# Half of the second key copy left out: fixed key tiles with zeroed rows in a two-layer hybrid decoder trunk

## The chip, the cores and the metric

The kernel runs on one core of one Trainium2 chip, in one launch. The metric is device time in microseconds (us). The time before is 1172.51 us, the median of three runs.

## The reference, cut to what matters

The model is a decoder trunk of two layers over 512 tokens of width 1024. In each layer an RMSNorm is followed by one input projection that feeds a short convolution, a causal differential attention and a Conformer convolution; their outputs are joined by an output projection, and a SwiGLU network follows. The change touches the attention alone. It has 4 heads, and each head has two maps (`m`) of 64-wide queries and keys:

```python
q = apply_rope(q.reshape(b, s, 2, N_DIFF_HEADS, DIFF_HEAD_DIM), cos, sin)
k = apply_rope(k.reshape(b, s, 2, N_DIFF_HEADS, DIFF_HEAD_DIM), cos, sin)
...
sc = jnp.einsum("bqmhd,bkmhd->bmhqk", qi, k, preferred_element_type=jnp.float32) * scale
p = jax.nn.softmax(jnp.where(mask, sc, -jnp.inf), axis=-1)
a = p[:, 0] - lam * p[:, 1]
return jnp.einsum("bhqk,bkhe->bqhe", a.astype(v.dtype), v)
```

Everything is float32. The kernel gets near that precision by splitting a factor into a high part (rounded to the matmul's own input type) and a low part (what the rounding left), and by adding products of the parts.

## The kernel before, in words

The activations lie transposed, 128 channels on the partitions by 512 tokens. Weights come from HBM in units of 512 KB (`raw`), each in two halves. ScalarE (ACT) copies a half to its high part, and the low part comes from VectorE (DVE, line 144 or 154) or, in the attention stretch, from ACT writing minus the high part (line 137) and a DMA from GpSimd (POOL, line 138) that adds the weights to it from HBM a second time. In that stretch POOL also issues the unit loads (line 118). Every engine works in the order in which the program names its instructions (`manual_schedule`), so a cast that waits for its weights holds back all that stands behind it on ACT.

The four heads go in two pairs, per layer. For each pair the projections give two PSUM tiles of queries (two halves of the rotary dimension, `ab`), then two of keys. `turn_qk` applies the rotary tables `cosr` and `sinr` on DVE; `split_and_pack` splits each result into the high and the low part (`hl`, 128 partitions by 2 by 512) and moves blocks of 32 partitions with DMAs from SyncE (SP) into the layout that the score matmuls want, line 450 for queries (`pq`) and line 448 for keys (`pk`). A pack is 16 DMAs in the order head of the pair (`hh`), `ab`, map (`m`), copy (`d`). Of a head's query tile the partitions 0 to 63 hold the high part and 64 to 127 the low part. Of a head's key tile both halves of the partitions hold the same: for each map a row group of high parts (`2 * m`) and one of low parts (`2 * m + 1`). So two matmuls give all four products (lines 489 and 490), and a third adds the causal mask (491):

```python
T.matmul(ps[:, m, :n], lhsT=q[:, m, qs], rhs=k[:, 2 * m, :n], start=True, stop=False)
T.matmul(ps[:, m, :n], lhsT=q[:, m, qs], rhs=k[:, 2 * m + 1, :n], start=False, stop=False)
```

There are four key packs in the program: layer 0 pair 0, layer 0 pair 1, layer 1 pair 0, layer 1 pair 1. Behind the keys of pair 0 comes the value projection (`values`): it fills four PSUM banks, ACT takes them out into `vt` (line 467), and the first scores of pair 0 need those banks. Behind the keys of pair 1 come the units of the short convolution (tiles `ax`, `ac`, `ab`) as filler, and the first scores of pair 1 need the first head's 8 DMAs of the pack. `slot` mixes scores, softmax, value products and two filler steps by hand.

At the start of the program POOL issues four DMAs that fetch `cosr` (line 697); DVE multiplies it by the norm's factor (line 703) before the first queries are turned.

Of the kernel before, what the change touches and what calls it, by code (L numbers as in the profile page):

```python
# [19 lines left out]
F32 = mybir.dt.float32  # L20
F32R = mybir.dt.float32r
# [7 lines left out]
S = 512  # L29
L = 2  # L30
P = 128
# [4 lines left out]
HD = 64  # L36
# [42 lines left out]
def trunk(ctx, tc, xT, pos, wu, cv, lamv, cst, out):  # L79
    nc = tc.nc  # L80
    V, A, G, T = nc.vector, nc.scalar, nc.gpsimd, nc.tensor

    def pool(name, bufs, **kw):
        return ctx.enter_context(tc.tile_pool(name=name, bufs=bufs, **kw))
    cp = pool("cp", 1)
# [4 lines left out]
    pk = pool("pk", 2)  # L90
# [125 lines left out]
    def start():  # L216


        nc.sync.dma_start(cvt, cv)
        nc.sync.dma_start(x[0], xT[0])  # L220
        load(0)
        nc.sync.dma_start(x[1], xT[1])
        load(1)
        nc.sync.dma_start(x[2], xT[2])
        nc.sync.dma_start(x[3], xT[3])
        load(2)
        nc.sync.dma_start(x[4], xT[4])
        ones_d = cp.tile([P, P], F32, name="ones_d")
        pi = pt.tile([P, P], I32, tag="t", name="posi")
        G.dma_start(pi, pos)  # L230
        lv = pt.tile([P, L, 4, HD], F32, tag="t", name="lv")
        G.dma_start(lv, lamv.partition_broadcast(P))
        G.dma_start(ones_d, cst[:, 1, :])
        cs = pt.tile([P, 2, P], F32, tag="t", name="cs")
        G.dma_start(cs, cst[:, 0::2, :])
        warm = sm.tile([P, 1], F32, tag="nm", name="warm")
        V.memset(warm, 0.0)
        A.activation(warm, warm, AF.Sin)

        wz = pt.tile([P, S], mybir.dt.bfloat16, tag="t", name="wz")  # L240
        V.memset(wz, 0.0)
        wp = tp.tile([P, S], F32, tag="tp", name="wp")
        for _ in range(10):
            T.matmul(wp, lhsT=wz[:, :P], rhs=wz, start=True, stop=True)
        ones_r = cp.tile([P, P], F32R, name="ones_r")
        idr = cp.tile([P, P], F32R, name="idr")
        maskr = cp.tile([P, P], F32R, name="maskr")
        G.tensor_copy(ones_r, ones_d)
        G.tensor_copy(idr, cs[:, 0, :])
        G.tensor_copy(maskr, cs[:, 1, :])  # L250
        consts.update(ones_d=ones_d, ones_r=ones_r, idr=idr, maskr=maskr, ident=idr.bitcast(F32), pi=pi, lv=lv)
# [6 lines left out]
    def make_h(k, gcol):  # L258

        g = cvt[:, gcol + k:gcol + k + 1]  # L260
        h = ph.tile([P, 2, S], F32R, tag="h", name=f"h{k}")
        A.activation(h[:, 0, :], x[k], AF.Copy, scale=g)  # L262
        V.scalar_tensor_tensor(h[:, 1, :], x[k], g, h[:, 0, :].bitcast(F32), ALU.mult, ALU.subtract)  # L263
        return h

    def add_square(k, run, eng, last=None):
        if run is None:
            run = pt.tile([P, S], F32, tag="t", name="run")
            A.activation(run, x[k], AF.Square)
            return run  # L270
        sq = pt.tile([P, S], F32, tag="t", name="sq")
        A.activation(sq, x[k], AF.Square)
        (V if (k == KC - 1 if last is None else last) else eng).tensor_add(run, run, sq)
        return run
# [69 lines left out]
    def rope_tables():  # L344

        p1, p2, p3 = _parts()
        w = pt.tile([P, 3, P], F32, tag="t", name="rt")
        ang, k, kl = (w[:, i, :] for i in range(3))
        kt = pt.tile([P, 3, P], F32R, tag="t", name="kh")
        kh = kt[:, 0, :]  # L350
        tab = kt[:, 1:3, :].bitcast(F32)
        cn, sn = tab[:, 0, :], tab[:, 1, :]
        V.tensor_copy(ang, consts["pi"])
        V.tensor_scalar(ang, ang, cvt[:, C_INV:C_INV + 1], None, ALU.mult)
        V.tensor_scalar(k, ang, 1.0 / TWO_PI, MAGIC, ALU.mult, ALU.add)
        V.tensor_scalar(k, k, -MAGIC, None, ALU.add)
        V.tensor_copy(kh, k)
        V.tensor_sub(kl, k, kh.bitcast(F32))
        yield
        for kk, p in ((kh.bitcast(F32), p1), (kl, p1), (kh.bitcast(F32), p2), (kl, p2), (k, p3)):  # L360
            V.scalar_tensor_tensor(ang, kk, -p, ang, ALU.mult, ALU.add)
        V.tensor_scalar(ang, ang, 3.1415925, -3.1415925, ALU.min, ALU.max)
        V.scalar_tensor_tensor(kl, ang, -1.0, ang, ALU.mult, ALU.min)
        yield
        A.activation(sn, ang, AF.Sin)
        A.activation(cn, kl, AF.Sin, bias=half_pi)
        dr = tc.dram_tile([32, 2, 4, P], F32, name="tab_dram")
        for b in range(4):
            (G, nc.sync)[b % 2].dma_start(dr[:, :, b, :], tab[32 * b:32 * b + 32, :, :])
        yield dr  # L370
# [14 lines left out]
            yield  # L385

    pending = []
    gates = []

    def later():  # L390
# [18 lines left out]
    def turn_qk(isk, ps, cosr, sinr, packs):  # L409

        t = [pt.tile([P, S], F32, tag="t", name=f"ro{i}") for i in range(4)]
        V.tensor_mul(t[0], ps[0], cosr)
        V.tensor_mul(t[1], ps[0], sinr)
        yield
        V.tensor_mul(t[2], ps[1], sinr)
        V.tensor_mul(t[3], ps[1], cosr)
        V.tensor_sub(t[0], t[0], t[2])
        V.tensor_add(t[1], t[1], t[3])
        if not packs:
            packs += [[pk.tile([P, n, S], F32R, tag=tag, name="p" + tag) for tag, n in (("q", 2), ("k", 4))]  # L420
                      for _ in range(2)]
        pending.append(functools.partial(split_and_pack, isk, t, packs))
        yield

    def split_and_pack(isk, t, packs):
        hls = [pr.tile([P, 2, S], F32R, tag="hl", name="hl") for _ in range(2)]
        for ab in range(2):
            if isk:
                A.copy(hls[ab][:, 0, :], t[ab])
            else:  # L430
                A.mul(hls[ab][:, 0, :], t[ab], QS)
        for ab in range(2):
            o, hl = t[ab], hls[ab]
            if isk:
                V.tensor_sub(hl[:, 1, :], o, hl[:, 0, :].bitcast(F32))
            else:
                V.scalar_tensor_tensor(hl[:, 1, :], o, QS, hl[:, 0, :].bitcast(F32), ALU.mult, ALU.subtract)
        for hh in range(2):
            q, k = packs[hh]
            for ab in range(2):  # L440
                hl = hls[ab]
                for m in range(2):
                    src = slice(64 * hh + 32 * m, 64 * hh + 32 * m + 32)
                    for d in range(2):
                        dst = slice(64 * d + 32 * ab, 64 * d + 32 * ab + 32)
                        eng = nc.sync
                        if isk:
                            eng.dma_start(k[dst, 2 * m:2 * m + 2, :].bitcast(F32), hl[src].bitcast(F32))
                        else:
                            eng.dma_start(q[dst, m, :].bitcast(F32), hl[src, d, :].bitcast(F32))  # L450

# [190 lines left out]
    def mixing(l, h, run, each):  # L642
# [3 lines left out]
        packs = [[], []]  # L646


        pq = [acc.tile([P, S], F32, tag="acc", name="qk") for _ in range(2)] if l == 0 else []
        pp = four("cc")  # L650

        def chunks(ks):
            for k in ks:
                w = next_half() if l else None
                for j, ps in enumerate(pq + pp):
                    c = slice(j * P, j * P + P)
                    mm3(ps, h[k], k == 0, k == KC - 1, w and (w[:, 0, c], w[:, 1, c]))
        if l == 0:
            start()

            hs = []

            def chunk(k):
                h.append(make_h(k, C_MIXG))
                if k:
                    hs.append(add_square(k - 1, hs[-1] if hs else None, V, True))
            rt = rope_tables()
            next(rt)
            prep(0, False)
            chunk(0)  # L670
            prep(1, False)
            chunk(1)
            next(rt)
            lam = lambdas()
            for k in range(6):
                lead[0] = (1, 2, 2, 3, 3, 3)[k]
                chunks([k])
                if k < 3:
                    nc.sync.dma_start(x[k + 5], xT[k + 5])
                chunk(k + 2)  # L680
                if k == 0:
                    state["tab"] = next(rt)
                if k == 1:
                    next(lam)
            hs.append(add_square(KC - 1, hs[-1], V, True))
            run = hs[-1]
            lead[0] = AHEAD - 1
        else:
            chunks(range(6))
# [237 lines left out]
    for l in range(L):  # L927
# [24 lines left out]
        for half in range(2):  # L952
            acts = []
            for f in range(FH):
# [8 lines left out]
                t = pt.tile([P, S], F32, tag="t", name="tg")  # L963
# [128 lines left out]
```

## Time and profile before

| | |
|---|---|
| median of 3 runs | 1172.51 us (1172.22 to 1177.48) |
| the profiled execution's own time | 1169.26 us |
| its span | 1167.4 us |
| PE (matmul) busy | 1137.1 us, 97% |
| DVE, ACT, POOL busy | 637.2, 502.6, 198.5 us |
| mean granted TensorE clock | 0.986 |
| DMA | 141.68 MB, mean 121 GB/s |

The profiled execution has 1.9 us outside its span. A busy share of 97% on PE counts the instructions from start to modelled end, at whichever clock they ran. The granted clock is 1.00 for 2.4 GHz and 0.50 for 1.2 GHz.

### The profile page before, as it was taken

The numbers are of one execution on the slowest core, as the hardware profiler recorded it, in microseconds if no ns is written. First come the engines' busy times: TensorE is split into PE (matmuls) and PEld (weight loads), VectorE is DVE, ScalarE is ACT, GpSimd is POOL, SyncE is SP. The second block draws the span as 40 slices with busy tenths as digits, with TensorE's granted clock in tenths as the row PEclk, the third lists the DMA queues.
The fourth block names the chain that finished last, engine by engine and source line by source line (L and its number), as shares of the span: only waits on it lengthen the run. The fifth ranks groups of instructions, "written<-read, shape, count | busy, mean of one in ns | idle before, by whom it ended". The sixth has DMA issues, their size and how long they took to land.

```text
span 1167.4 us, 14339 instructions
## 1 busy us (share of the span) xinstructions
PE 1137.1 (97%) x5238; PEld 943.8 (81%) x5238; DVE 637.2 (55%) x1140; ACT 502.6 (43%) x1034; POOL 198.5 (17%) x229
## 2 busy tenths in 40 slices
PE   8989899999999999999999899999999999999995
PEld 6878787788888888888888788877888888888885
DVE  6777786654443344444448788657444333444445
ACT  6546566643332233333334467765333222333323
POOL 2222223311100011010112222332111000011001
PEclk9989899999999999999999899999999999999998
DMA  7785847432332322322337878663223223223212
GB/s 228 190 211 130 197 109 165 106 126 91 104 95 90 109 91 94 105 90 99 102 98 177 195 170 190 139 158 97 102 90 106 93 91 108 91 94 105 90 55 73
DMA packets 50342, 141.68 MB, mean 121 GB/s; under 512 B 7104, under 2 KB 9408, under 8 KB 50272
## 3 DMA queue, kind: packets, MB, share of 16 engines
q1 hardware_dynamic: 29888, 88.79, 23.7%
q0 software_dynamic: 20384, 51.98, 19.5%
q8 instruction: 41, 0.67, 0.2%
q14 instruction: 29, 0.24, 0.1%
HBM read 125.93 MB, written 2.23 MB: 110 GB/s over the span
## 4 chain that ended last, share of the span: by engine, by line
PE 85%; DMA 4%; DVE 4%; issue 3%; ACT 2%; SPq 1%; POOL 1%; DVEq 0%; ACTq 0%; POOLq 0%
PE od L186 8%; PE od L188 8%; PE od L187 8%; PE gp L188 7%; PE gp L187 7%; PE up L187 7%; PE up L188 7%; PE up L186 7%; PE gp L186 6%; PE qk L186 3%; DMA raw<-wu 2%; PE qk L187 2%; PE qk L188 2%; PE cc L186 1%; PE cc L187 1%
## 5 line engine op out<-in xcount | busy, mean ns | idle before, releaser
L135 ACT CAST w<-raw 128x512 fp32r<-128x512 f32 x384 | 237.6, 622 | 495.1 <-PE od L188 146.0
L144 DVE TENSOR_TENSOR w<-raw,w 128x512 fp32r<-128x512 f32 x265 | 187.1, 707 | 239.8 <-ACT w L135 239.2
L966 POOL TENSOR_TENSOR tg<-tg,r 128x512 f32<-128x512 f32 x44 | 57.8, 1316 | 520.3 <-ACT tg L965 510.7
L187 PE MATMUL gp<-h,w 128*128 128x512 f32 x352 | 137.2, 390 | 0.6 <-DVE h L263 0.6
L186 PE MATMUL up<-h,w 128*128 128x512 f32 x352 | 137.2, 390 | 0.1
L188 PE MATMUL gp<-h,w 128*128 128x512 f32 x352 | 137.1, 390 | 0.0
L186 PE MATMUL gp<-h,w 128*128 128x512 f32 x352 | 137.1, 390 | 0.0
L187 PE MATMUL up<-h,w 128*128 128x512 f32 x352 | 137.0, 389 | 0.0
L188 PE MATMUL up<-h,w 128*128 128x512 f32 x352 | 137.0, 389 | 0.0
L186 PE MATMUL od<-act,w 128*128 128x512 f32 x328 | 127.6, 389 | 0.0
L187 PE MATMUL od<-act,w 128*128 128x512 f32 x328 | 127.6, 389 | 0.0
L188 PE MATMUL od<-act,w 128*128 128x512 f32 x328 | 127.6, 389 | 0.0
L138 POOL DMA_DIRECT2D w<-wu x82 | 72.7, 887 | 240.0 <-ACT w L137 217.9
L578 DVE SCALAR_TENSOR_TENSOR acc<-pad,cvt,acc 128x511 f32<-128x511 f32 (+14 forms) x120 | 88.0, 734 | 2.8
L187 PEld LDWEIGHTS gp<-h,w 128*128 128x128 f32 x352 | 66.1, 188 | 15.1 <-DVE h L263 1.5
L186 PEld LDWEIGHTS up<-h,w 128*128 128x128 f32 x352 | 66.1, 188 | 14.6 <-DVE x L932 1.0
L186 PEld LDWEIGHTS gp<-h,w 128*128 128x128 f32 x352 | 66.1, 188 | 14.1 <-ACT h L262 0.5
L188 PEld LDWEIGHTS up<-h,w 128*128 128x128 f32 x352 | 66.1, 188 | 13.8
L188 PEld LDWEIGHTS gp<-h,w 128*128 128x128 f32 x352 | 66.1, 188 | 13.6
L187 PEld LDWEIGHTS up<-h,w 128*128 128x128 f32 x352 | 66.1, 188 | 13.6
L188 PEld LDWEIGHTS od<-act,w 128*128 128x128 f32 x328 | 61.6, 188 | 12.9
L187 PEld LDWEIGHTS od<-act,w 128*128 128x128 f32 x328 | 61.6, 188 | 12.7
(255 smaller groups left out, 1982.0 us busy)
## 6 DMA issues: line engine op xcount, KB each, us to landing
raw<-wu SPq DMA_DIRECT2D x135, 512.0 KB, 3.5
raw<-wu POOLq DMA_DIRECT2D x56, 512.0 KB, 6.0
w<-wu POOLq DMA_DIRECT2D x82, 256.0 KB, 4.8
pk<-hl SPq DMA_DIRECT2D x64, 128.0 KB, 6.3
pq<-hl SPq DMA_DIRECT2D x64, 64.0 KB, 3.7
x<-xT SPq DMA_DIRECT2D x8, 256.0 KB, 7.5
yT<-fo SPq DMA_DIRECT2D x8, 256.0 KB, 2.5
raw<-wu SPq DMA_DIRECT2D x2, 256.0 KB, 4.9
```

What stands on the lines that cost most here:

```text
L135: A.copy(t[:, 0, :], raw)
L138: G.dma_start(t[:, 1, :], wu[u, :, 4 * P * half:4 * P * half + 4 * P], accum_op=ALU.add)
L144: sub()
L186: T.matmul(ps, lhsT=hi, rhs=rh[:, 0, :], start=first, stop=False)
L187: T.matmul(ps, lhsT=hi, rhs=rh[:, 1, :], start=False, stop=False)
L188: T.matmul(ps, lhsT=lo, rhs=rh[:, 0, :], start=False, stop=last)
L578: V.scalar_tensor_tensor(a[:, d:], pad[:, :S - d], cvt[:, c - d:c - d + 1], a[:, d:], ALU.mult, ALU.add)
L966: G.tensor_mul(t, t, r)
```

## The change

The key tiles are no longer taken from a rotating pool for every pair: two fixed tiles, one for each head of a pair, serve all four packs. Once, at the start of layer 0, POOL writes zeros into the low-part rows of the lower copy (partitions 64 to 127, row group `2 * m + 1`), four memsets of 64 partitions by 512. The second copy of the keys (`d == 1`) then moves only the high part: 8 of the 16 DMAs of a pack carry 32 rows of 2 KB, 64 KB, where they carried 32 rows of 4 KB, 128 KB. The score matmuls are the same in number and shape. What they no longer add is the product of the queries' low part with the keys' low part.

```diff
     pending = []
+
+    keys = [cp.tile([P, 4, S], F32R, name=f"pk{hh}") for hh in range(2)]
+
+    def zero_rows():
+        for t in keys:
+            for m in range(2):
+                G.memset(t[HD:, 2 * m + 1, :].bitcast(F32), 0.0)
     gates = []
...
         if not packs:
-            packs += [[pk.tile([P, n, S], F32R, tag=tag, name="p" + tag) for tag, n in (("q", 2), ("k", 4))]
-                      for _ in range(2)]
+            packs += [[pk.tile([P, 2, S], F32R, tag="q", name="pq"), keys[hh]] for hh in range(2)]
...
-                        if isk:
+                        if isk and d == 0:
                             eng.dma_start(k[dst, 2 * m:2 * m + 2, :].bitcast(F32), hl[src].bitcast(F32))
+                        elif isk:
+                            eng.dma_start(k[dst, 2 * m, :].bitcast(F32), hl[src, 0, :].bitcast(F32))
                         else:
                             eng.dma_start(q[dst, m, :].bitcast(F32), hl[src, d, :].bitcast(F32))
...
             hs.append(add_square(KC - 1, hs[-1], V, True))
             run = hs[-1]
+            zero_rows()
             lead[0] = AHEAD - 1
```

## Rows read from the trace of the kernel before

**Rows 1.** Waits of PE: total us, times, longest us

```profile
PE ps L489 <- ACT vt L467: 7.3, 2, 4.2
PE ps L489 <- DMA pk<-hl: 5.6, 2, 4.4
```

**Rows 2.** Timeline of PE, first score matmul after each pack [idle before <-releaser]

```profile
80.08 0.48 PE L489 MATMUL ps<-pk,pq 128*128 128x128 f32 x1 [4.21 <-ACT vt L467]
...
135.25 0.45 PE L489 MATMUL ps<-pk,pq 128*128 128x128 f32 x1 [4.42 <-DMA pk<-hl]
...
653.62 0.47 PE L489 MATMUL ps<-pk,pq 128*128 128x128 f32 x1 [3.14 <-ACT vt L467]
...
705.39 0.30 PE L489 MATMUL ps<-pk,pq 128*128 128x128 f32 x1 [1.19 <-DMA pk<-hl]
```

**Rows 3.** Stretches behind them: us, engines' busy us (count), PEclk, DMA share, GB/s

```profile
80.10:86.80 6.70, 6.70 (x20) 5.57 (x21) 3.21 (x7) 2.93 (x8) 1.35 (x2) 0.52 0.92 223
...
135.25:141.40 6.15, 6.15 (x18) 4.88 (x19) 3.92 (x8) 2.46 (x7) 0.85 (x1) 0.52 0.98 239
...
653.60:660.30 6.70, 6.68 (x20) 5.58 (x21) 3.34 (x8) 2.97 (x8) 1.39 (x2) 0.52 1.05 259
...
705.40:712.20 6.80, 6.80 (x37) 5.65 (x38) 6.38 (x12) 3.71 (x11) 1.91 (x3) 1.00 1.08 270
```

**Rows 4.** Timeline of ACT, last cast ahead of the value copies of layer 0

```profile
77.73 0.62 ACT L135 CAST w<-raw 128x512 fp32r<-128x512 f32 x1 [2.54 <-DMA raw<-wu]
```

**Rows 5.** Chain of waits: start us, us, what

```profile
66.53 11.05 DMA raw<-wu
...
641.13 9.98 DMA raw<-wu
```

**Rows 6.** DMA queues, 60.6 to 80.5 us, key pack: packets, MB, share of engines

```profile
DMA  0079799189599999779999999999999999999989
...
q1 hardware_dynamic: 768, 2.10, 41.0%
```

**Rows 7.** The same for 104.5 to 120.5 us, a query pack

```profile
q1 hardware_dynamic: 768, 1.05, 24.9%
```

**Rows 8.** Timeline of SP's queue up to 70.5, 128, 643 us; two last issues alone

```profile
60.60 10.82 SPq L448 DMA_DIRECT2D pk<-hl  x12
...
69.95 1.48 SPq L448 DMA_DIRECT2D pk<-hl  x1
...
121.17 7.49 SPq L448 DMA_DIRECT2D pk<-hl  x8
...
634.91 8.65 SPq L448 DMA_DIRECT2D pk<-hl  x10
...
641.38 2.18 SPq L448 DMA_DIRECT2D pk<-hl  x1
```

**Rows 9.** The 12th, 8th and 10th DMA of these packs: KB, us to landing

```profile
pk<-hl SPq DMA_DIRECT2D x1, 128.0 KB, 7.7
...
pk<-hl SPq DMA_DIRECT2D x1, 128.0 KB, 8.1
...
pk<-hl SPq DMA_DIRECT2D x1, 128.0 KB, 10.2
```

**Rows 10.** DMAs that met little other traffic, issued at 117.85 and 60.60 us

```profile
pq<-hl SPq DMA_DIRECT2D x1, 64.0 KB, 2.0
...
pk<-hl SPq DMA_DIRECT2D x1, 128.0 KB, 2.3
```

**Rows 11.** POOL: a group of 512 columns, and the timeline at the start

```profile
L966 POOL TENSOR_TENSOR tg<-tg,r 128x512 f32<-128x512 f32 x44 | 57.8, 1316 | 520.3 <-ACT tg L965 510.7 <-DVE w L144 9.6
...
38.87 0.57 POOL L118 DMA_DIRECT2D raw<-wu  x1 [8.17 <-ACT w L135]
```

**Rows 12.** Landing of `cosr` at the start, and its first use on DVE

```profile
cosr<-tab_dram POOLq DMA_DIRECT2D x4, 64.0 KB, 6.5
...
40.81 0.69 DVE L703 TENSOR_TENSOR cosr<-cosr,r 128x512 f32<-128x512 f32 x1 [1.35 <-ACT r L340]
```

## The prediction

> **What bounds the kernel now.** PE does: it is busy for 97% of the span, so only time in which PE stands still or runs slowly can be won. I read four views in turn. First the list of PE's waits: only two kinds of long wait touch the attention, both at the first score matmul behind a key pack [rows 1]. The timeline of PE gives the four places and sizes: 4.21, 4.42, 3.14 and 1.19 us, 12.96 us in all [rows 2]. Then the stretches behind them: after the first three the granted clock is 0.52, which is 1.2 GHz for nearly all of 6.7, 6.15 and 6.7 us, and PE does in that time half of what it does at 2.4 GHz. So each of these waits costs again half of its stretch: 3.35, 3.08 and 3.35 us, 9.8 us in all. Behind the wait of 1.19 us the clock stayed at 1.00 [rows 3]. Together the four places cost 22.7 us, 1.9% of the time. That is all that this change can touch on PE.
>
> What ends them? In pair 1 of both layers it is the key pack itself. In pair 0 the wait is put down to the copy of the values on ACT (`vt`); but in front of that copy ACT stood for 2.54 us in a weight cast whose unit (`raw`) had not landed [rows 4], and the chain of waits runs through that load: 11.05 us in layer 0 and 9.98 in layer 1, from issue to landing [rows 5]. The load is not urgent for PE. It is late because the DMA engines are full: the queue view of 60.6 to 80.5 us shows busy tenths of 9 from about 66 us on, and the key pack's queue alone holds 41.0% of sixteen engines there [rows 6]. So all four places wait, directly or around one corner, for the same thing, DMA engines that a key pack keeps busy.
>
> **The change part by part.** *The halved DMAs.* A pack still has 16 DMAs and 512 packets of data, one for each row; 8 DMAs have packets of 2 KB where they had 4 KB. What a packet costs is in two rows. A key pack of 4 KB packets takes 41.0% of 16 engines for 19.9 us, 130.5 engine-us [rows 6]; a query pack, with as many packets of 2 KB, takes 24.9% of 16 engines for 16.0 us, 63.7 engine-us [rows 7]. Halving all 512 packets would save 66.8 engine-us; halving 256 saves 33.4, or 2.09 us of all sixteen engines per pack, 0.26 us per halved DMA. (Half the bytes are half the engine time, so there is no fixed price per packet that would eat the gain.)
>
> What of it lies ahead of each wait? In the order of a pack every second DMA is a halved one.
> - Layer 0, pair 0: the load that ACT waits for lands at 66.53 + 11.05 = 77.58 us. SP's row up to 70.5 us holds 12 DMAs of the pack; the 12th is issued from 69.95 us on [rows 8] and lands 7.7 us later [rows 9], with the load. So 12 DMAs, 6 halved, were served beside it: 6 x 0.26 = 1.6 us sooner.
> - Layer 0, pair 1: the first scores need the head's 8 DMAs, 4 halved: 1.05 us sooner. The 8th takes 8.1 us to land [rows 9].
> - Layer 1, pair 0: the load lands at 651.1 us; the 10th DMA (issued at 641.38, 10.2 us [rows 8, 9]) lands behind it at 651.6. So 9 were ahead, 4 halved: 1.05 us.
> - Layer 1, pair 1: again 4 halved, 1.05 us, of a wait of 1.19.
>
> Sum of the waits: 1.6 + 1.05 + 1.05 + 1.05 = 4.75 us. Each has a bound on both sides. Below: nothing, if SP, whose issues are held up now (the 12th of the first pack took 1.48 us and the 10th of the third 2.18 [rows 8]), posts the later DMAs of the pack sooner and the packets that they put in front of the load use up what the halves saved. Above: ACT's own waits for the loads, 2.54 us in layer 0 [rows 4] and no more than the 3.14 us of PE in layer 1, and all of the 4.42 and 1.19 us where the pack itself is awaited and a freed issue counts too: 11.3 us.
>
> *The clock.* The waits left would be 2.6, 3.4, 2.1 and 0.1 us. The rows show a fall behind 3.14 us and none behind 1.19 [rows 2, 3]; nothing shows what lies between. Going by the nearer row, 3.4 and 2.6 still bring a fall, and 2.1 (0.9 from 1.19, 1.0 from 3.14) just does not. So I take one fall as gone, that of layer 1 pair 0: 3.35 us. Ends: no fall gone (0) and all three gone (9.8).
>
> *The memsets.* Four on POOL, ahead of the four DMAs that fetch `cosr`. No row shows a memset of this size; the nearest of 512 columns is a POOL product at 1.316 us [rows 11], so 5.3 us for four is my upper end and close to 0 the lower; I take 2.5. POOL has 8.17 us of idle time behind the `cosr` issues, up to 38.87 [rows 11], so its weight loads do not move. The `cosr` issues end at 38.87 - 8.17 = 30.7 us; the last starts some 0.6 us before that and, at 6.5 us, lands at about 36.6, where DVE uses it at 40.81 [rows 12]. At 2.5 us the tables still come 1.7 us early. At 5.3 they come about 1.1 us late, and what is late then is the turning of the first queries on DVE, while PE works on the keys in other banks: nothing, or 1.1 us at worst.
>
> *The fixed tiles.* They take the place of two buffers of the same size, used in the same turn. Pair 1's packs are issued after the last scores of pair 0 have run, since the query pack ahead of them in the queue needs those too. Cost nothing; a DMA that waited longer there would show as a later start of the key packs, up to the length of that wait. The second score matmul has the same shape, so its time stands.
>
> Sum: 4.75 + 3.35 = 8.1 us. Of the profiled execution's own 1169.26 us that leaves 1161.2. The median shown is 1172.51, 3.3 us higher, and the same step from there gives 1164.4 us.
>
> **A rule against it.** With little traffic a key DMA of 128 KB landed in 2.3 us and a query DMA of 64 KB in 2.0 [rows 10]; by these alone a halved DMA lands 0.3 us sooner, four places win 1.2 us and no fall of the clock goes away. The Trainium skill says this more sharply (page "DMA: Bandwidth & Descriptors", section "Anatomy of one DMA — SWDGE (gpsimd) path"): a transfer costs about 2.0 us plus its bytes at 436 GB/s, most of it the receipt of the last write. By that fit, which is an estimate here, 64 KB less is 0.15 us, and four places would win 0.6 us. The rows say that the packs do not land in this regime: under load the same 128 KB take 7.7 to 10.2 us [rows 9], so 5 to 8 us of it are queueing.
>
> **The rivals.**
> - *Nothing lands sooner* (0.20): the landing is latency, or SP's freed issues fill the gap. For it: the rows of quiet DMAs. Against it: full engines. Win 0 to 1.2 us: 1171 to 1172.5.
> - *The transfers shrink, but every clock fall stays* (0.17): 4.75 us, 1167.8. For it: 3.14 us was enough for a fall, and 2.1 may be.
> - *Two or three falls go away* (0.22): 4.75 + 6.4 to 4.75 + 9.8 us, 1158 to 1161. For it: each wait has upper ends above my values.
> - *Slower: the memsets hold up the tables* (0.06). Place: POOL at 28 to 31 us. It decides when one memset takes over (40.81 - 36.6) / 4 = 1.05 us, and reaches PE only when DVE is late by several us more. At three times the POOL product, 4 us each, the tables come 12 us late; with a fall of the clock behind it that costs some 10 us, and if it takes the wins with it, 1179 to 1182. Against it: a memset reads nothing, and the product that I measure it by reads two tiles.
>
> **How the numbers follow.** The forecast itself has 0.35. The measurement of this kernel tells about 0.5% (5.9 us) from no change. Forecast and two or three falls are faster by more than that: 0.57. Nothing sooner and all falls staying are within it: 0.37. Slower: 0.06. The range reaches from 1156, a little under the case of three falls with the waits at their middle, to 1173.5, a little over no change; it leaves out the wins at all upper ends at once (below) and the memsets (above), about 1.5 in 10. The forecast's own range, one fall with the waits between half and one and a half of their sum, is 1162 to 1167.
>
> **What the changed profile would show.** The key queue with 1.57 MB for 2.10 in each pack and, over the same work, some 97 engine-us for 130; the two loads landing in about 9.5 and 9 us; waits at the first scores near 2.6, 3.4, 2.1 and 0.1 us; a granted clock of 1.00 behind the third; memsets on POOL well under 1.3 us each and no wait of DVE for `cosr`. I am wrong on the mechanism if the packs' engine time does not shrink, or if it does and the loads land as late as before; and on the size if the falls of the clock do not follow the length of the waits.

## The result and the profile after

The changed kernel takes 1161.64 us in the median of four runs (1160.02 to 1161.96), against 1173.11 us for the kernel before (1172.22 to 1177.48): a ratio of 0.9897, with a 95% interval of 0.9865 to 0.9930. That is 1.0% faster. The forecast was 1164.4 us in a range of 1156 to 1173.5.

First the timeline of PE, at the four places of [rows 2], with the idle time ahead of each first score matmul in brackets, and one row behind the fourth place:

```profile
80.43 0.33 PE L497 MATMUL ps<-pk,pq 128*128 128x128 f32 x1 [3.45 <-ACT vt L475]
...
132.69 0.35 PE L497 MATMUL ps<-pk,pq 128*128 128x128 f32 x1 [3.09 <-DMA pk<-hl]
...
649.07 0.33 PE L497 MATMUL ps<-pk,pq 128*128 128x128 f32 x1 [2.58 <-ACT vt L475]
...
697.07 0.30 PE L497 MATMUL ps<-pk,pq 128*128 128x128 f32 x1 [0.43 <-DMA pk<-hl]
...
703.51 0.33 PE L524 MATMUL pT<-idr,e 128*128 128x128 f32 x1 [0.60 <-DVE yb L562]
```

The same four waits stand there, put down to the same releasers, each shorter: 4.21 became 3.45, 4.42 became 3.09, 3.14 became 2.58 and 1.19 became 0.43. That is 3.4 us less, of 12.96. The last row is a new short wait that was hidden before.

The stretches behind the first three, read as [rows 3] (length, busy times, granted clock, DMA):

```profile
80.40:85.10 4.70, 4.67 (x17) 3.81 (x18) 4.15 (x9) 2.96 (x8) 0.54 (x1) 0.64 0.97 248
...
132.70:136.60 3.90, 3.90 (x12) 3.24 (x13) 2.71 (x7) 2.46 (x7) 0.00 (x0) 0.56 1.09 255
...
649.10:655.80 6.70, 6.70 (x36) 5.76 (x37) 5.59 (x13) 4.58 (x15) 1.34 (x2) 1.00 0.80 185
```

What a slow stretch takes from PE is its length times what the clock lacks. Before that was 6.70 x 0.48, 6.15 x 0.48 and 6.70 x 0.48, 9.4 us. Now it is 4.70 x 0.36 and 3.90 x 0.44, 3.4 us, and nothing behind the third place: PE does 36 matmuls in the 6.70 us in which it did 20. So the clock gave back 6.0 us at these places, more than the waits themselves.

The DMA queues while the first key pack is moved, 61.7 to 79.6 us, to be held against [rows 6]:

```profile
DMA  0057667579798999994999699999999999999998
...
q1 hardware_dynamic: 768, 1.57, 32.4%
...
pk<-hl SPq DMA_DIRECT2D x8, 128.0 KB, 5.2
pk<-hl SPq DMA_DIRECT2D x8, 64.0 KB, 5.2
```

The pack has as many packets as before, 1.57 MB for 2.10, and takes 32.4% of 16 engines for 17.9 us: 92.8 engine-us, where it took 130.5. That is 2.36 us of all sixteen engines per pack.

The chain of waits shows the two loads of [rows 5] again, and the timeline of ACT the cast that waits for the first of them, as in [rows 4]:

```profile
67.68 10.24 DMA raw<-wu
...
637.13 9.43 DMA raw<-wu
```

```profile
78.07 0.62 ACT L135 CAST w<-raw 128x512 fp32r<-128x512 f32 x1 [2.19 <-DMA raw<-wu]
```

Last the start: the timeline of POOL, and the first use of `cosr` on DVE.

```profile
28.34 0.54 POOL L118 DMA_DIRECT2D raw<-wu  x1 [6.53 <-DVE w L154]
...
30.57 1.93 POOL L394 MEMSET pk<- 64x512 f32 x4
32.45 1.02 POOL L706 DMA_DIRECT2D cosr<-tab_dram  x2
...
41.91 0.69 DVE L712 TENSOR_TENSOR cosr<-cosr,r 128x512 f32<-128x512 f32 x1 [1.35 <-ACT r L340]
```

The four memsets take 1.93 us together. DVE's first use of `cosr` waits 1.35 us for ACT's `r`, as before, and not for the table.

The profiled span fell by 7.3 us. The list adds up to about that: 3.4 from the waits and 6.0 from the clock, less 0.6 for the new wait and 1.1 that the start took longer. That 1.1 us is PE's distance at the first place: it came there at 80.43 - 3.45 = 76.98 us and before at 80.08 - 4.21 = 75.87. It does not come from the memsets: the POOL issue well ahead of them, at 28.34 us, stood at 26.48 us before. The medians lie 11.5 us apart, more than the two profiled executions, because the one of before was among its quicker ones: in the rounds of the experiments the unchanged kernel took anything from 1164.67 to 1179.65 us.

### The profile page after: what moved, and what is told of

It reads as the page before. It is cut to its first block, busy times and chain, and to the rows that moved or that the text cites. A ratio compares the mean times of both kernels' runs of the same rounds, so it can differ in the third digit from the quotient of the medians.

```text
span 1160.1 us, 14343 instructions
## 1 busy us (share of the span) xinstructions
PE 1132.7 (98%) x5238; PEld 939.0 (81%) x5238; DVE 637.0 (55%) x1140; ACT 503.0 (43%) x1034; POOL 200.3 (17%) x233
## 3 DMA queue, kind: packets, MB, share of 16 engines
HBM read 125.93 MB, written 2.23 MB: 110 GB/s over the span
## 4 chain that ended last, share of the span: by engine, by line
PE 84%; DMA 4%; DVE 4%; issue 3%; ACT 2%; SPq 1%; POOL 1%; DVEq 0%; ACTq 0%; POOLq 0%
PE od L186 8%; PE od L187 8%; PE od L188 8%; PE gp L187 7%; PE gp L188 7%; PE up L187 7%; PE up L188 7%; PE up L186 7%; PE gp L186 7%; DMA raw<-wu 3%; PE qk L186 2%; PE qk L188 2%; PE qk L187 2%; PE cc L188 1%; PE o L539 1%
## 5 line engine op out<-in xcount | busy, mean ns | idle before, releaser
L186 PEld LDWEIGHTS up<-h,w 128*128 128x128 f32 x352 | 66.1, 188 | 14.6 <-DVE x L941 1.0
```

The source lines that it names most:

```text
L186: T.matmul(ps, lhsT=hi, rhs=rh[:, 0, :], start=first, stop=False)
```

## Experiments

The theory: a halved transfer frees time of the DMA engines; what waits for them, the pack itself in pair 1 and a weight load in front of the value copies in pair 0, lands sooner; PE waits less; and where it waits less the clock falls less. Rivals: that the fixed tiles do it, or the clock by chance, or one place alone.

**Fixed tiles alone (e1).** Both copies moved whole, no memsets:

```diff
-                        if isk and d == 0:
+                        if isk:
                             eng.dma_start(k[dst, 2 * m:2 * m + 2, :].bitcast(F32), hl[src].bitcast(F32))
-                        elif isk:
-                            eng.dma_start(k[dst, 2 * m, :].bitcast(F32), hl[src, 0, :].bitcast(F32))
...
-            zero_rows()
```

> The fixed tiles stay, both copies of the keys are moved whole again (128 KB each) and the memsets go. Theory (the halved transfers free DMA engines, so the waits at the first scores shorten and with them the slow stretches of TensorE): back at the time of before, 1172 us within 3, key pack's queue at 2.10 MB per pack, waits of about 4.2, 4.4, 3.1 and 1.2 us. Rival (the fixed tiles do it, because tiles from the rotating pool carry waits): stays at about 1161.6 us with waits near those of the changed kernel, 3.5, 3.1, 2.6 and 0.4.

Measured: 1172.81 us against 1171.32, a ratio of 1.0011 (0.9980 to 1.0042). Its timeline of PE at the four places:

```profile
81.01 0.33 PE L495 MATMUL ps<-pk,pq 128*128 128x128 f32 x1 [4.25 <-DMA pk<-hl]
...
135.02 0.45 PE L495 MATMUL ps<-pk,pq 128*128 128x128 f32 x1 [4.79 <-DMA pk<-hl]
...
654.78 0.48 PE L495 MATMUL ps<-pk,pq 128*128 128x128 f32 x1 [3.83 <-ACT vt L473]
...
709.50 0.45 PE L495 MATMUL ps<-pk,pq 128*128 128x128 f32 x1 [3.94 <-DMA pk<-hl]
```

Within the interval of 0.4% the fixed tiles are worth nothing, and that rival is out. Two things more are to be seen. In pair 0 of layer 0 the pack itself came last this time, 4.25 us: the pack and the value copies behind the load end close together, and either can be the later. (The cast began at 78.66 us in this execution; the 2.35 us that its work takes, worked out under e3, end at 81.01 us too.) And the fourth wait is 3.94 us where the profiled execution of before had 1.19, so waits of whole packs scatter by microseconds from one execution to the next. That fits the wide spread of the kernel before; that it is the whole of it is not shown.

**All transfers halved (e2).** The low parts of the keys are moved nowhere and their rows are zero in both copies, which leaves out one more product:

```diff
-                        if isk and d == 0:
-                            eng.dma_start(k[dst, 2 * m:2 * m + 2, :].bitcast(F32), hl[src].bitcast(F32))
-                        elif isk:
+                        if isk:
                             eng.dma_start(k[dst, 2 * m, :].bitcast(F32), hl[src, 0, :].bitcast(F32))
...
-                G.memset(t[HD:, 2 * m + 1, :].bitcast(F32), 0.0)
+                G.memset(t[:, 2 * m + 1, :].bitcast(F32), 0.0)
```

> The low parts of the keys are moved nowhere: all 16 DMAs of a pack are 64 KB and the low row groups are zero in both copies, so the product of the queries' high part with the keys' low part is left out too. Theory: another 2.1 us of sixteen engines per pack; the waits shrink about as much again, to some 2.8, 1.8, 2.0 and 0, and a second clock fall may go: 1155 to 1159 us. Rival (most of the gain came from the clock falling differently by chance, not from the transfers): 1161 us within 2, with waits as in the changed kernel.

Measured: 1155.36 us (1154.31 to 1155.74), a ratio of 0.9857 (0.9823 to 0.9891). From its list of PE's waits, those of the attention (total us, times, longest):

```profile
PE pT L522 <- DVE yb L560: 2.5, 2, 1.2
PE ps L495 <- ACT vt L473: 2.1, 1, 2.1
...
PE pT L522 <- DVE e L513: 0.5, 1, 0.5
```

Of the four waits one is left, 2.07 us in pair 0 of layer 0, fewer than the 2.8, 1.8 and 2.0 us that I expected. With whole copies, half of them halved and all of them halved the time goes 1172.8, 1161.6, 1155.4 us (the middle one from other rounds; as ratios to before 1.0011, 0.9897, 0.9857): the more is halved, the faster the kernel. The executions of the halved kernels lie closer together, though they are fewer, and what shows next is a wait for DVE at the transposes.

**The cast behind the value copies (e3, e4).** The late load is wanted by one cast that PE does not need for a long time. These two kernels move that one cast behind the copies, in the changed kernel and in the kernel before:

```diff
             if n % 4 == 3:
                 each(n // 4)
+            if n == 27:
+                held.append(None)
...
             vt.append(t[:, b % 2, :])
+        release()
         return vt
```

> The changed kernel, with the one weight cast that waits for the late load moved behind the four copies of the values on ACT. Theory (in pair 0 the first scores wait for ACT only because ACT stands in that cast): the two waits on the value copies fall from 3.5 and 2.6 us to under 0.7, no fall of the clock behind them, the waits on the key pack stay near 3.1 and 0.4: 5 to 8 us faster than the changed kernel, 1154 to 1157 us. Rival (the key pack of pair 0 itself is what comes last there, or the cast is late for its own users): the waits stay above 2 us under another name, 1160 to 1163 us.

Measured: 1157.57 us (1155.81 to 1158.52), a ratio of 0.9877 (0.9847 to 0.9907).

```profile
PE pT L527 <- DVE e L518: 3.3, 2, 2.3
PE ps L500 <- DMA pk<-hl: 1.8, 1, 1.8
```

> The same move of the cast in the kernel before, with whole copies and rotating tiles. Theory: the two waits of 4.2 and 3.1 us fall under 1 us without any change of a transfer, their two falls of the clock go, the waits on the pack stay at 4.4 and 1.2: about 12 us faster than before, 1160 us within 3. Rival (the transfers of the pack themselves end last in pair 0): a wait for the pack of 2 us or more takes their place, 1166 us or more.

Measured: 1163.20 us (1159.71 to 1166.96), a ratio of 0.9939 (0.9912 to 0.9965).

In both, the waits on the value copies are gone from PE's list or under 0.9 us, with no transfer changed: it was ACT standing in that cast. How much of the wait that is can be read from rows. The first score matmul follows the start of the cast by 2.35 us at both places of pair 0 before: 80.08 - 77.73 and 653.62 - 651.26.

```profile
651.26 0.62 ACT L135 CAST w<-raw 128x512 fp32r<-128x512 f32 x1 [2.32 <-DMA raw<-wu]
```

Those 2.35 us are the cast, the negated copy and two value copies: work of ACT that a faster transfer starts sooner and does not shorten. PE came to these places at 75.87 and 650.48 us, so of its 4.21 and 3.14 us only 1.86 and 0.78 went by before the cast began.

In neither kernel was the full price won. In e4 the waits on the pack of pair 1 are 5.00 and 3.69 us, longer than the 4.4 and 1.2 that I expected. In e3 they are 1.78 us and none, shorter than the 3.1 and 0.4 that I expected, but a new wait of 2.27 us stands at the first transpose of layer 0, for DVE's product `e`: DVE spends 8.4 us in convolution taps that the value projection had queued, and the first row maximum stands behind them.

```profile
73.45 8.42 DVE L589 SCALAR_TENSOR_TENSOR acc<-pad,cvt,acc 128x499 f32<-128x499 f32 x11
81.78 0.42 DVE L504 TENSOR_REDUCE nm<-ps 128x2 f32<-128x256 f32 x1
```

**Halving pair 1 alone (e5).** The packs of pair 0 whole, those of pair 1 halved (which leaves low parts of pair 0 in the lower rows when pair 1 is computed):

```diff
+        packed[0] += isk
...
-                        if isk and d == 0:
+                        if isk and (d == 0 or packed[0] % 2):
```

> The changed kernel, with the packs of pair 0 whole again in both layers and those of pair 1 halved; the lower rows of low parts then hold pair 0's when pair 1 is computed, so the small product of low parts differs. Theory: each pack acts at its own place. The waits on the value copies go back to about 4 and 3 us with their clock falls, those on the pack stay at about 3.1 and 0.4: 1166 us within 3, between the two kernels. Rival (one place carries the whole gain): at 1161.6 us if it is pair 1, at 1171 if it is pair 0.

Measured: 1165.77 us (1159.82 to 1167.70), a ratio of 0.9937 (0.9909 to 0.9966): between the two. The waits were 5.39 and 2.74 us on the value copies and 3.36 on the pack in layer 0; in layer 1 there was none on the pack above 0.3. Each pack acts where it stands. By the ratios pair 1 alone is worth 0.6%, where the whole change is worth 1.0% (0.8% in e10 below). That pair 0 has a part too is seen in its waits; the intervals overlap, so how the gain divides is not settled.

**What is left (e6, e7, e8).** Three kernels build on e3. e6 puts four filler steps ahead of pair 1's first scores; e7 moves eight taps from the value projection into pair 0's slots; e8 does both.

```diff
+        fill(4)
         for b in range(8):
             slot((pairs[1], b), (0, 2, 2, 2, 2, 2, 0, 2)[b], None if b else head(1))
```

```diff
-        vt = values(h, rT, lambda n: tap(3))
+        vt = values(h, rT, lambda n: tap(2))
...
-            slot((pairs[0], b), 1)
+            slot((pairs[0], b), 2)
```

> The changed kernel with the cast behind the value copies, and with four more filler steps (2.7 us of matmuls) ahead of pair 1's first scores, taken from the later slots. Theory (what is left at pair 1's first scores is a wait for transfers, which any other work of PE hides): the wait of 1.8 us goes, and PE is 2 to 4 us faster there; the slots at the end of pair 1 lose four steps and give back 0 to 3 us: 1154 to 1158 us against 1157.6. Rival (PE then waits for the softmax of the last slots as long as it saved): 1157.6 us within 1, with a new wait at the end of pair 1.

Measured: 1161.74 us (1158.60 to 1162.58), a ratio of 0.9904 (0.9873 to 0.9936). The wait on the pack fell to 1.02 us, but the slots at the end of pair 1 now wait for the softmax, in both layers:

```profile
167.96 0.30 PE L527 MATMUL pT<-idr,e 128*128 128x128 f32 x1 [1.09 <-DVE e L518]
...
733.24 0.30 PE L527 MATMUL pT<-idr,e 128*128 128x128 f32 x1 [1.08 <-DVE e L518]
```

Behind each stands a further 0.68 us, and behind the second the clock fell as well, to 0.71 over the next 5.8 us. The medians put e6 4 us above e3, each in rounds of its own and with intervals that overlap. The theory's gain did not come. The rival's new wait did, at a higher price than the rival named, which was no change within 1 us.

> The changed kernel with the cast behind the value copies, and with eight of the convolution's taps moved from the value projection into pair 0's slots, one more per slot. Theory (with the cast moved, DVE's queue of taps became the next limit: the first row maximum waits behind them and PE stands for 2.3 us at the first transpose): that wait falls under 0.7 us, 1 to 3 us faster, 1154.5 to 1156.5 us. Rival (the taps only move, and each slot's chain over DVE grows by 0.75 us): other waits at the transposes take its place, 1157.6 us within 1.

Measured: 1153.67 us (1152.75 to 1155.11), a ratio of 0.9844 (0.9798 to 0.9890): the fastest kernel that computes all that the changed kernel does, and a little faster than the 1154.5 to 1156.5 us that I expected. The transposes' wait for DVE's `e` is gone, and the list of waits in the attention is

```profile
PE ps L500 <- DMA pk<-hl: 3.2, 2, 2.9
PE pT L527 <- DVE yb L565: 0.9, 1, 0.9
```

> Both of these moves together. Theory: their gains add, 1152 to 1156 us, and no wait above 1 us is left in the attention. Rival: no faster than the better of the two.

Measured: 1158.73 us (1157.00 to 1159.25), a ratio of 0.9881 (0.9843 to 0.9920): slower than e7 in the same rounds, with no execution of one among those of the other. The filler costs at the end of pair 1 here too (1.09 and 1.08 us at the same transposes, with a granted clock of 0.72 and 0.73 in the 6 us behind them), and the gains do not add.

**What the halved transfers are worth in the better order (e9), and the changed kernel again (e10).** e9 is the kernel before with the cast and the taps moved as in e7; e10 is the changed kernel unedited.

> The kernel before, with whole copies and rotating tiles, and with the two moves of the fastest kernel so far: the cast behind the value copies and eight taps in pair 0's slots. Theory (the halved transfers are worth what their engine time costs at waits that PE still sees; with pair 0's waits gone by order, only pair 1's are left): waits on the pack of 4 to 5 and 1 to 4 us with a clock fall or two, about 1160 us within 3, so that the halved transfers are worth some 6 us there, where they were worth some 10 to 11. Rival (the order alone gives all of it): 1153.7 us within 2.

Measured: 1163.46 us (1160.39 to 1164.59), a ratio of 0.9921 (0.9897 to 0.9946). The waits on the whole packs of pair 1, which e7 has at 2.93 us and nearly none:

```profile
128.76 0.44 PE L492 MATMUL ps<-pk,pq 128*128 128x128 f32 x1 [5.01 <-DMA pk<-hl]
...
695.93 0.44 PE L492 MATMUL ps<-pk,pq 128*128 128x128 f32 x1 [5.13 <-DMA pk<-hl]
```

By the ratios, the halved transfers are worth 0.9921 - 0.9844 = 0.8% here, some 9 us. I had expected 6, which the two intervals do not exclude. Once pair 0 no longer holds PE up, pair 1's whole packs cost more in this profile than in that of before: 5.01 and 5.13 us for 4.42 and 1.19, with a granted clock of 0.69 for 5.3 us and 0.55 for 6.8 us behind them. The order alone does not give the gain; the rival is out.

> The changed kernel once more, unedited, on the same chip and in the same rounds. Theory: 1161.6 us within 2, waits at the first scores of about 3.5, 3.1, 2.6 and 0.4 us, a spread over its executions of 2 us or so. Rival (that the first measurement of it was lucky with the clock): 1165 us or more, with a spread like that of the kernel before, some 10 us.

Measured: 1162.62 us (1161.25 to 1165.44), a ratio of 0.9923 (0.9894 to 0.9952). The gain repeats, a little smaller, within the first one's interval. The waits were 2.35, 2.19, 1.90 and 0.29 us, shorter than in the first profile. The time was not, for the clock took 6.80 x 0.48 and 5.00 x 0.34, 5.0 us, behind the first two places (3.4 in the first profile) and a further 1.7 us behind the attention of layer 0, at small matmuls that do not wait for a pack:

```profile
190.00:196.20 6.20, 6.20 (x24) 5.02 (x24) 2.79 (x17) 3.16 (x7) 1.44 (x3) 0.72 0.44 119
```

In the first place the load was no longer late at all. The cast began as PE finished its value matmuls, and the 2.35 us that are left are ACT's own:

```profile
76.83 0.62 ACT L135 CAST w<-raw 128x512 fp32r<-128x512 f32 x1 [2.51 <-PE v L466]
```

## Why the prediction was right, step by step

**The bound and the way the waits come about: shown.** The four waits shrank; PE's other long waits stayed as they were (3.4, 1.7, 1.6 and 1.2 us in the lists of both), and what came or went beside them is 0.6 us or less. That pair 0 waits for a load around the corner of ACT is shown by e3 and e4, which remove those waits without touching a transfer. Two things the prediction did not say: 2.35 us of each wait of pair 0 is ACT's own work behind the load, so the order holds more of it than the transfers do; and the pack itself can come last there as well (e1).

**The price of a packet: right, a little low.** I took 2.09 us of sixteen engines per pack; 2.36 were freed.

**The waits: right in kind, the sizes loose.** The forecast was 1.6, 1.05, 1.05 and 1.05 us, 4.75 in all. The first profile shows 0.76, 1.33, 0.56 and 0.76, 3.4 in all; the repeat (e10) shows 1.86, 2.23, 1.24 and 0.90, 6.2 in all. So the forecast lies between two executions of the same kernel, and the terms of pair 0 came to half in one and above their size in the other. The loose step is the count of DMAs ahead of the load, which I took over from before. The lower bound that I had named is what happened in part in the first profile: SP was held up less and posted the pack sooner, as its queue shows (the first issue of the first pack, the 13th and the last), with the landing of the 13th:

```profile
61.73 0.51 SPq L454 DMA_DIRECT2D pk<-hl  x1
...
70.22 1.49 SPq L454 DMA_DIRECT2D pk<-hl  x1
...
73.02 0.60 SPq L456 DMA_DIRECT2D pk<-hl  x1
...
pk<-hl SPq DMA_DIRECT2D x1, 128.0 KB, 7.4
```

Sixteen issues take 11.9 us where they took 14.6. The 13th, issued at 70.22 us, lands 7.4 us later, just ahead of the load at 67.68 + 10.24 = 77.92. So 13 of the DMAs were served beside the load and not 12, and the load took 0.8 us less, not 1.6. In e10 the load was issued earlier against the pack, 5.4 us behind its first DMA for 5.95, and took 9.2 us, so that it landed at 76.7 us. The pack's 11th DMA landed only behind it, at 68.96 + 8.2 = 77.2:

```profile
67.49 0.82 POOL L118 DMA_DIRECT2D raw<-wu  x1
...
raw<-wu POOLq DMA_DIRECT2D x1, 512.0 KB, 9.2
...
68.96 1.20 SPq L454 DMA_DIRECT2D pk<-hl  x1
...
pk<-hl SPq DMA_DIRECT2D x1, 128.0 KB, 8.2
```

So the count was 10 there, and the wait 1.86 us shorter. The size of this term changes with the count from one execution to the next; that the count is the whole of the difference was not tried by itself.

**The clock: the size was too small.** I let one fall of three go, 3.35 us. The third went, as forecast and in the repeat too, but the two that I kept came back shorter: 6.0 us in all, and 4.4 in the repeat. The step assumed that a slow stretch is there whole or not at all; it can also be about half as long.

**The memsets and the fixed tiles: right.** 1.93 us for four memsets, where I took 2.5, with no wait for the tables behind them; and a ratio of 1.0011 for the fixed tiles (e1).

**The sum.** In the first profile waits too large by 1.35 us and the clock too small by 2.6 cancel in part. In the repeat both terms were too small, and a fall of the clock elsewhere took some of it back. From the median before, the forecast was 1164.4; it came out at 1161.64 and, repeated, 1162.62. That it came so close is thus partly luck: the terms of one execution differ from those of the next by more than the forecast differs from the median. The rule against the change, that a transfer costs mostly a fixed latency, is answered by e2 and by the 13th DMA: under load these transfers take 5 to 8 us to land (medians of 5.2, and 7.4 for the 13th), and the time follows what the engines carry.

## What to carry to other kernels

When the matmul engine waits, follow the wait past the engine that is named: here ACT was named, a weight cast in front of it held it, and a full set of DMA engines held that. Bytes that the result can do without cost time where the DMA engines are full just then and something urgent waits behind them. The price per packet from two queue rows of the same kernel was a good price for them here (2.09 us per pack against 2.36). Before removing bytes, look also at what stands in the queue in front of the awaited work, since moving one cast and eight taps was worth about another 8 us (1161.6 to 1153.7, in different rounds); and work put ahead of a wait is taken from where it hid another.

## What the runs showed of the hardware

The granted clock does not follow the length of the wait alone. Behind 2.93 us of idle PE it stayed at 1.00 (e7), behind 2.35 us it was 0.52 for 6.8 us (e10, second row):

```profile
126.90:133.70 6.80, 6.80 (x37) 5.72 (x38) 5.82 (x11) 3.77 (x11) 0.85 (x1) 1.00 0.93 220
```

```profile
79.20:86.00 6.80, 6.80 (x21) 5.67 (x22) 5.05 (x10) 2.94 (x8) 1.35 (x2) 0.52 0.79 220
```

It also fell where PE had not waited a microsecond at a time. In e2, with small matmuls, short waits and 3.13 us busy of 4, PE is followed by a stretch at 0.57:

```profile
743.00:747.00 4.00, 3.13 (x19) 2.26 (x17) 1.50 (x2) 2.01 (x4) 1.59 (x3) 1.00 1.03 224
747.00:751.00 4.00, 4.00 (x14) 3.18 (x14) 2.79 (x17) 1.18 (x4) 0.68 (x1) 0.57 0.67 165
```

So a forecast can give a fall only a chance, and the gain of a shortened wait scatters by the microseconds of a fall. What decides it stays open. The memset of 64 partitions by 512 on POOL, which no row of before showed, took some 0.5 us, well under the product of 512 columns at 1.316 us that I had bounded it by.
